# Re-dealt rows of the triangular inverses, rotation of two heads at once, split first loads and another stage order in a hybrid decoder block

## The chip, the cores and the metric

The kernel runs on one core of one Trainium2 chip. The metric is the device time of one execution in microseconds (us). TensorE (PE) does matrix products into PSUM; VectorE (DVE), ScalarE (ACT) and GpSimd (POOL) do everything else; transfers between HBM and on-chip memory (SBUF) are issued from the queues of SyncE (SP) and ScalarE.

## The reference

One decoder layer in float32, sequence 2048, model width 1024:

```
n    = rmsnorm(h);  proj = n @ w_in           # q,k,v,gate,a,b of 4 DeltaNet heads; q,k,v,gate of 4 retention heads
gdn:  silu(causal conv4(q,k,v)); l2norm(q), l2norm(k); chunks:
      T = (I + tril(beta k k^T * decay))^-1;  u = T v_beta - (T k_beta) S;  o = q S + (q k^T * decay) u;  S = d S + k^T u
ret:  q,k = rotary(q), rotary(k);  o = (q k^T * D) v + (q xi) R;  R = g R + (k zeta)^T v
mix  = [rms(o_gdn) * w * silu(gate), rms(o_ret) * silu(gate)]
h    = h + mix @ w_out
h    = h + (silu(g) * u) @ w_down,   g,u = causal conv3(rmsnorm(h) @ w_up)      # inner width 2816
out  = rmsnorm(h)
```

All heads are 128 wide. The rotary step multiplies a head's 128 columns by a cosine row and adds the columns with each two neighbours exchanged, times a sine row.

## The kernel before, in words

**Products.** Every float32 factor is split into a high and a low part, and a product runs as three passes: high·high, high·low, low·high (lines 116 to 118 in mm3; 399 to 401 in the token-major projections, tokmajor). The out projection (product, "wo") and the two MLP products are additionally done as seven half-size block products with sums instead of eight.

**Blocks and stages.** The sequence is cut in four blocks of 512 tokens, of four chunks of 128 each. Each block has some sixty mixer stages, named by a letter in ORDER (lines 41 to 51), which writes out their order by hand; a digit ahead is the block:

- pro: first norm. pro2 loads xT tiles (L382, on SP's queue) and scales each half into a high and a low part (L387 ScalarE, L388 VectorE); pro1 loads x and sums squares. load_chunk brings weights (L293 on SP), splits them (L295 ScalarE, L296 VectorE) and stores the split form in HBM for later blocks; `len(uses) > NLATE` leaves that out for the first NLATE chunks at their first use.
- k0, q0, kq, v0: the retention projections. rotate (L764 to L774) applies the rotary step per token tile and head pair: per head two VectorE products (L769, L771) out of PSUM and one POOL addition (L774).
- a, f: DeltaNet projections of a head; c: its k k^T and q k^T products (kk, L585) and the stores of the 32x32 diagonal blocks to HBM (z1, L621, on ScalarE's queue); e: v transposed; d, dec: decays.
- b0, b1: gdn_base, the inverses of the 32x32 diagonal blocks for a pair of heads. Nb is loaded from z1 (L628, SP), so that each of the 128 partitions holds one whole block. Each block is inverted by columns: POOL runs 31 times a product (L637) and an addition (L639). A block's 32 rows lie on four partitions, eight rows on each, and all eight are touched at every column. The result goes out to HBM as z2 in one 128 KB store (L641, SP), comes back in eight loads into a block-diagonal tile AT (L648, SP) and is transposed by VectorE into NT (L650).
- l0, l1: products that build the full 128x128 inverse from the 32x32 ones (yps, L665, is their first); r00 to r13: the recurrent steps of a pair of heads, chunk by chunk (gdn_rec: ks L714 → kv on VectorE L717 → wps L724 → u on VectorE L727 → sps L732 → state on VectorE L734).
- h, y: a retention head (rr L818, state steps L810, transposes L826, rkk L832; output ro L846, evacuated by ScalarE as o at L849, squares, power on POOL L857).
- p: gate projections (tokmajor again; ScalarE evacuates into mix, L412); g, G: o times norm and gate (VectorE, L435), transposed by TensorE (mxt, L437) and combined (co, L440 to L445).
- W1 to W7: the seven out-projection products (ScalarE and VectorE split the factor, L917 and L918; wo); N: second norm, transposed and stored to HBM (L952, L953).

The MLP follows: its input tiles xr are loaded from what N stored (SP, L985) and split by ScalarE (L973); the first tiles are prepared while block 3's mixers still run.

**What sets the order.** Each engine runs its instructions in one queue of its own, in program order. The program order comes from ORDER and, within and around it, from the framework's scheduler, which places instructions by their dependences. Tiles are drawn from pools; the numbers of buffers stand in BUFS and in NVR, NACC, NPB, NXR and others (lines 16 to 39). The pools' tiles share the bytes of SBUF as they come free, so a tile can wait for the last reader of another tile that lay there before it. The framework adds these waits.

**Constants.** cols (norm and conv weights), rows and masks (identity, triangle, and eye8, the start of the inverses) are loaded on ScalarE's queue (L95, L243, L248) at the start.

Of the kernel before, what the change touches and what calls it, by code (L numbers as in the profile page):

```python
# [10 lines left out]
AF = mybir.ActivationFunctionType  # L11
ALU = mybir.AluOpType
# [7 lines left out]
NVR = 4  # L20
# [4 lines left out]
NACC = 9  # L25
# [4 lines left out]
NPB = 11  # L30
# [3 lines left out]
NLATE = 3  # L34
NXR = 7
FD = 5
BUFS = {"n1": 8, "ykq": 5, "kv": 4, "NT": 6, "AT": 8, "o": 4, "n2s": 11, "xk": 2, "og": 1, "co": 7, "Cw": 7,
        "wx": 1, "wsq": 2, "wvr": 3, "wvt": 8, "ca": 8, "mix": 10, "D": 8, "rk": 6, "rq": 3, "rv": 8,
        "Ar": 1, "Nb": 7, "rot": 1, "rrow": 7}

ORDER = ("0pro 0k0 0v0 0dec 0d0 0a0 0c0 0f0 0e0 0q0 0d1 0a1 0c1 0f1 0a2 0e1 0d2 0c2 0f2 0h0 0y0 0b0 0h1 "
# [10 lines left out]
P = 128  # L52
S = 2048
D = 1024
KT = D // P
TB = 512
NB = S // TB
NT = TB // P
# [25 lines left out]
def hybrid_block(ctx, tc, x, xT, w_kq, w_v, w_g, w_rk, w_r0, w_r, w_o, w_u, w_d, cols, rows, fnr, masks, rot, out):  # L84
    nc = tc.nc
# [9 lines left out]
    nc.scalar.dma_start(colt, cols)  # L95
# [123 lines left out]
def mixers(ctx, tc, base, base_used, marks, drp, mm3, gamma, mhalf, n1w, n2w, gcw, gv127, epsr, gnw, n2d, hd,  # L219
# [28 lines left out]
    nc.scalar.dma_start(mk, masks)  # L248
# [6 lines left out]
    DVE.tensor_scalar(below, U, 1.0, 1e4, op0=ALU.subtract, op1=ALU.mult)  # L255
# [21 lines left out]

    def load_chunk(key, src):
        first = key not in uses
# [6 lines left out]
        for o in range(0, n, step):  # L286
# [3 lines left out]
            else:  # L290
                if o % (2 * step) == 0:
                    raw2 = unit(wp, "wraw", [P, 2, step], bufs=NRAW)
                    marks["w"] = nc.sync.dma_start(raw2.rearrange("p a n -> p (a n)"), src[:, o:o + 2 * step])  # L293
# [61 lines left out]
    def A_items(b, st):  # L355
# [22 lines left out]
        def pro2(_):  # L378
            st["n1"] = []
            for kk in range(4):  # L380
                xk = unit(ap_, "xk0", [P, 2, TB], bufs=4) if b == 0 else al("xk", [P, 2, TB])
                nc.sync.dma_start(xk.rearrange("p a t -> p (a t)"), xT[b, kk])  # L382
                for i in range(2):
# [3 lines left out]
                    ACT.activation(n1[:, 0], xk[:, i], AF.Copy, scale=n1w[:, k:k + 1])  # L387
# [237 lines left out]
        def gdn_base(p):  # L625
            def f(_):
# [8 lines left out]
                for j in range(31):  # L635
                    n = 31 - j
                    POOL.tensor_tensor(tm[:, :, :n], Nb[:, j:j + 1, j + 1:].to_broadcast([P, 8, n]),  # L637
                                      X[:, :, j:j + 1].to_broadcast([P, 8, n]), op=ALU.mult)
                    POOL.tensor_tensor(X[:, :, j + 1:], X[:, :, j + 1:], tm[:, :, :n], op=ALU.add)  # L639
                z2 = drp.tile([2, NT, 4, 32, 32], F32, tag="z2", name="z2")  # L640
                nc.sync.dma_start(z2.rearrange("h c k (g a) i -> (h c k g) (a i)", g=4), X.rearrange("p c i -> p (c i)"))  # L641
# [116 lines left out]
        def rot_dst(p, which):  # L758
            dst = [half(st, ("rt", p, which), "r" + which, i) for i in range(2)]
            for i in range(2):  # L760
                st["rh", 2 * p + i, which] = dst[i]
# [573 lines left out]
```

## Time and profile before

| | us |
|---|---|
| runs | 2462.69, 2459.72, 2457.21 |
| median | 2459.72 |
| span of the profiled execution | 2458.5 |
| TensorE busy | 2397.2 |
| VectorE busy | 1596.7 |
| ScalarE busy | 998.8 |
| POOL busy | 532.7 |

The profile is of one further execution; for it there is the span, from its first to its last instruction. Rows of instructions read: start in us, duration in us, engine, line, operation, output<-inputs, partitions x elements, count, and in brackets how long the engine was idle before and what released it. Rows of waits read: engine, tile and line that waited <- engine, tile and line that released it: us in all, times, longest. Rows of groups read: line, engine, operation, out<-in, shape, count | busy us, mean ns of one | idle us before them and what ended it. Rows of DMA kinds end with the size of one and the median us from issue to landing. The mixers of the four blocks end at about 1225 us; the rest is the MLP.

### The profile page before, as it was taken

To read this page: it belongs to the slowest core of one execution; us is meant where nothing else is said; L and a number is where in the kernel's file an instruction comes from. 1 tells how busy PE (TensorE), PEld (TensorE's weight loads), DVE (VectorE), ACT (ScalarE), POOL (GpSimd) and SP (SyncE) were. 2 spreads that over 40 slices of the span, in tenths; PEclk is the share of its full clock that TensorE was granted. 3 is DMA by queue.
4 is the path that set the end of the run, shared out by engine and by line. 5 is a ranking of instruction groups with operands and counts; after the bars stand their busy time and mean duration, and the time that the engine had idled before them with its cause. 6 is when DMAs were issued, how large, how long until landed. Compare 5 with 4: busy or idle time off the path is not lost.

```text
span 2458.5 us, 35801 instructions
## 1 busy us (share of the span) xinstructions
PE 2397.2 (98%) x12476; PEld 2016.0 (82%) x12476; DVE 1596.7 (65%) x3157; ACT 998.8 (41%) x2152; POOL 532.7 (22%) x877
## 2 busy tenths in 40 slices
PE   8998899999999999998999999999999999999998
PEld 7887788788888878887888888888888888888887
DVE  5855777444754563447888988896556577454674
ACT  6644535344442552336454344442122234332341
POOL 1354245621047105240000000000000002421030
PEclk9999999999999999999999999999999999999999
DMA  8856589674765656654998878877667778775773
GB/s 327 277 187 218 214 310 343 223 247 175 268 228 180 211 186 222 224 184 181 349 365 313 303 290 300 290 280 250 233 239 258 270 259 281 243 224 156 220 242 112
DMA packets 287477, 607.29 MB, mean 247 GB/s; under 512 B 41088, under 2 KB 121152, under 8 KB 287296
## 3 DMA queue, kind: packets, MB, share of 16 engines
q1 hardware_dynamic: 270720, 590.70, 68.7%
q10 hardware_dynamic: 16576, 14.30, 1.9%
q8 instruction: 98, 1.61, 0.3%
q14 instruction: 83, 0.68, 0.1%
HBM read 405.32 MB, written 199.59 MB: 246 GB/s over the span
## 4 chain that ended last, share of the span: by engine, by line
PE 84%; POOL 5%; DMA 4%; DVE 3%; issue 2%; ACT 2%; SPq 0%; ACTq 0%; POOLq 0%; DVEq 0%
PE p L116 11%; PE p L118 11%; PE p L117 11%; PE d L118 6%; PE d L116 6%; PE d L117 6%; PE tok L399 4%; PE tok L401 4%; PE tok L400 4%; PE chm L116 3%; PE chm L117 3%; PE chm L118 3%; POOL pers L639 2%; POOL pers L637 2%; PE wo L116 2%; PE wo L117 2%
## 5 line engine op out<-in xcount | busy, mean ns | idle before, releaser
L117 PE MATMUL p<-x,wu 128*128 128x512 f32 x1176 | 457.7, 389 | 0.0
L116 PE MATMUL p<-x,wu 128*128 128x512 f32 x1176 | 452.7, 389 | 0.0
L118 PE MATMUL p<-x,wu 128*128 128x512 f32 x1176 | 450.0, 389 | 0.0
L399 PE MATMUL tok<-wc,n 128*128 128x512 f32 (+2 forms) x768 | 276.5, 365 | 19.5 <-ACT n L387 9.6
L400 PE MATMUL tok<-wc,n 128*128 128x512 f32 (+2 forms) x768 | 276.6, 361 | 1.1 <-DVE wc L296 1.1
L401 PE MATMUL tok<-wc,n 128*128 128x512 f32 (+2 forms) x768 | 275.1, 361 | 0.0
L116 PEld LDWEIGHTS p<-x,wu 128*128 128x128 f32 x1176 | 220.8, 188 | 46.4 <-DVE uc L1053 0.4
L118 PEld LDWEIGHTS p<-x,wu 128*128 128x128 f32 x1176 | 220.8, 188 | 45.8
L117 PEld LDWEIGHTS p<-x,wu 128*128 128x128 f32 x1176 | 220.8, 188 | 45.8
L1095 DVE SCALAR_TENSOR_TENSOR acc<-uc,base,acc 128x1023 f32<-128x1023 f32 (+1 forms) x176 | 221.0, 1280 | 39.2 <-ACT acc L1092 38.9
L1053 DVE TENSOR_TENSOR uc<-p,uc 128x512 f32<-128x512 f32 x224 | 153.6, 689 | 134.8 <-PE p L118 131.6
L186 POOL TENSOR_TENSOR vt<-vr 128x512 f32<-128x512 f32 x44 | 66.0, 1504 | 633.0 <-DMA vr<-in_w_d 465.8
L399 PEld LDWEIGHTS tok<-wc,n 128*128 128x128 f32 x768 | 146.1, 191 | 41.0 <-ACT n L387 9.6
L117 PE MATMUL d<-v,uu 128*128 128x512 f32 x448 | 174.3, 389 | 0.0
L118 PE MATMUL d<-v,uu 128*128 128x512 f32 x448 | 174.3, 389 | 0.0
L116 PE MATMUL d<-v,uu 128*128 128x512 f32 x448 | 174.3, 389 | 0.0
L400 PEld LDWEIGHTS tok<-wc,n 128*128 128x128 f32 x768 | 146.5, 191 | 20.8 <-DVE wc L296 1.5
L401 PEld LDWEIGHTS tok<-wc,n 128*128 128x128 f32 x768 | 145.3, 191 | 19.8
L116 PE MATMUL chm<-n,wc 128*128 128x512 f32 x384 | 151.7, 395 | 0.0
L118 PE MATMUL chm<-n,wc 128*128 128x512 f32 x384 | 151.2, 394 | 0.0
L117 PE MATMUL chm<-n,wc 128*128 128x512 f32 x384 | 150.8, 393 | 0.0
L1092 ACT ACTIVATE acc<-uc,base 128x1024 f32<-128x1024 f32 x88 | 97.2, 1144 | 86.2 <-DVE uc L1053 45.1
(250 smaller groups left out, 4723.3 us busy)
## 6 DMA issues: line engine op xcount, KB each, us to landing
wu<-wu SPq DMA_DIRECT2D x308, 512.0 KB, 5.9
wc<-wd SPq DMA_DIRECT2D x168, 512.0 KB, 5.2
wv<-wo SPq DMA_DIRECT2D x84, 512.0 KB, 5.2
wd<-wc SPq DMA_DIRECT2D x60, 512.0 KB, 4.8
ur<-au SPq DMA_DIRECT2D x56, 512.0 KB, 5.5
wur<-in_w_u SPq DMA_DIRECT2D x44, 512.0 KB, 6.5
au<-st SPq DMA_DIRECT2D x88, 256.0 KB, 4.7
vr<-in_w_d SPq DMA_DIRECT2D x77, 256.0 KB, 5.0
```

The lines of the kernel that those rows point to most:

```text
L116: PE.matmul(ps, ah, bh, start=(first and i == 0), stop=False, skip_group_check=chk)
L117: PE.matmul(ps, ah, bl, start=False, stop=False, skip_group_check=chk)
L118: PE.matmul(ps, al, bh, start=False, stop=(i == n - 1), skip_group_check=chk)
L186: POOL.tensor_tensor(tt[:, j], a, b_, op=ALU.subtract)
L399: PE.matmul(ps, ah, wh, start=(k == 0), stop=False)
L400: PE.matmul(ps, ah, wl, start=False, stop=False)
L401: PE.matmul(ps, al_, wh, start=False, stop=(k == KT - 1))
L637: POOL.tensor_tensor(tm[:, :, :n], Nb[:, j:j + 1, j + 1:].to_broadcast([P, 8, n]), X[:, :, j:j + 1].to_broadcast([P, 8, n]), op=ALU.mult)
L639: POOL.tensor_tensor(X[:, :, j + 1:], X[:, :, j + 1:], tm[:, :, :n], op=ALU.add)
L1053: add = lambda o, ps, a: DVE.tensor_tensor(o, ps, a, op=ALU.add)
L1092: ACT.activation(acc, u, AF.Copy, scale=mcw[:, ci, 2:3])
L1095: DVE.scalar_tensor_tensor(acc[:, t:], u[:, :T2 - t], w, acc[:, t:], op0=ALU.mult, op1=ALU.add)
```

## The change

It has four parts.

1. **Inverse.** The 32 rows of a block are dealt to its four partitions in turn (row = 4a + g on partition g) instead of in runs of eight. At column j only the first j//4 + 1 of the eight places can hold anything but zero, and only these are multiplied and added. eye8 is dealt the same way. The z2 store becomes four, one for each g, of 32 KB in pieces of 32 numbers.
2. **Rotation.** Both heads of a pair at once: three VectorE instructions of 256 columns for each token tile and pair, the addition among them, in place of four of 128 on VectorE and two on POOL.
3. **First loads.** The first weight chunk and the first xT tile come in halves, interleaved on SP's queue; cols in a piece of 8 columns and the rest; the masks are issued behind the scale of the fourth half tile. NLATE goes from 3 to 4.
4. **Order.** A new ORDER string, and other buffer numbers. The MLP's code is the same, with NACC 9 to 8 and NXR 7 to 6.

```diff
--- before.py
+++ after.py
@@ -17,38 +17,38 @@
 LA = 1
 NHH = 5
 NUU = 14
-NVR = 4
+NVR = 5
 NVV = 23
 NWUR = 2
 NST = 4
 NUC = 6
-NACC = 9
+NACC = 8
 NWU = 9
 NWV = 5
 FX = (0, 2, 4, 1, 5)
 NU = 4
-NPB = 11
+NPB = 8
 NPM = 4
 NPR = 2
 NRAW = 3
-NLATE = 3
-NXR = 7
+NLATE = 4
+NXR = 6
 FD = 5
-BUFS = {"n1": 8, "ykq": 5, "kv": 4, "NT": 6, "AT": 8, "o": 4, "n2s": 11, "xk": 2, "og": 1, "co": 7, "Cw": 7,
-        "wx": 1, "wsq": 2, "wvr": 3, "wvt": 8, "ca": 8, "mix": 10, "D": 8, "rk": 6, "rq": 3, "rv": 8,
-        "Ar": 1, "Nb": 7, "rot": 1, "rrow": 7}
-
-ORDER = ("0pro 0k0 0v0 0dec 0d0 0a0 0c0 0f0 0e0 0q0 0d1 0a1 0c1 0f1 0a2 0e1 0d2 0c2 0f2 0h0 0y0 0b0 0h1 "
-         "0y1 0d3 0e2 0a3 0c3 0f3 0e3 0l0 0r00 0r01 0r02 0b1 0r03 0l1 0r10 0kq 0r11 0p1 0h2 0r12 0y2 "
-         "0r13 1pro 0p0 0g0 1k0 0h3 0G0 0y3 1dec 0g1 0G1 0W1 1d0 1a0 1c0 1f0 1e0 0W2 1a3 1q0 0W6 0W7 1d1 "
-         "1a1 1c1 1f1 1e1 1d3 1c3 0W5 1f3 1e3 1v0 0W3 1h1 1y1 1b0 1a2 0W4 1d2 1c2 1f2 1e2 1h0 1y0 1l0 0N "
-         "1kq 1r00 1r01 1r02 1b1 1h2 1y2 1r03 1p1 1p0 1l1 1r10 2pro 1h3 1y3 1r11 1g1 1r12 1r13 1g0 2k0 "
-         "1G1 2dec 1G0 2v0 1W1 1W2 2d0 2d2 2a0 2c0 2f0 2e0 1W6 1W7 2a2 1W5 1W3 2c2 2a1 2f2 2f1 2e2 1W4 "
-         "2d1 2c1 2e1 2b0 2q0 2h1 2y1 2d3 2a3 2c3 2f3 2b1 2e3 2h0 2y0 2l0 2r00 2r01 2p0 2r02 2r03 2l1 "
-         "2r10 2r11 2r12 2kq 2r13 2p1 1N 3pro 2g0 2h2 2y2 3k0 2h3 2y3 2G0 2g1 2G1 3dec 3d0 3a0 3c0 3f0 "
-         "3d1 3e0 2W1 2W2 2W6 3a2 3a1 3c1 3f1 3e1 2W7 3q0 3v0 3b0 3h0 3y0 2W5 3d2 3d3 3h1 3c2 3f2 3e2 "
-         "2W3 3a3 3c3 3kq 3y1 3f3 3e3 3p0 3l0 3r00 3r01 3r02 3r03 3h2 3y2 3b1 3l1 3r10 3r11 3r12 3r13 "
-         "3g0 2W4 3p1 3G0 2N 3h3 3y3 3g1 3G1 3W1 3W2 3W6 3W7 3W5 3W3 3W4 3N")
+BUFS = {"n1": 8, "ykq": 5, "kv": 5, "NT": 6, "AT": 9, "o": 7, "n2s": 16, "xk": 2, "og": 4, "co": 7, "Cw": 6,
+        "wx": 1, "wsq": 5, "wvr": 3, "wvt": 8, "ca": 7, "mix": 7, "D": 4, "rk": 8, "rq": 2, "rv": 9, "Ar": 1,
+        "Nb": 8, "rot": 1, "rrow": 8}
+
+ORDER = ("0pro 0k0 0v0 0dec 0d0 0a0 0c0 0f0 0e0 0d1 0a1 0c1 0f1 0a2 0e1 0q0 0d2 0f2 0h0 0c2 0y0 0b0 0h1 "
+         "0y1 0d3 0e2 0a3 0c3 0f3 0e3 0l0 0r00 0r01 0r02 0r03 0b1 0l1 0kq 0r10 0r11 0r12 0h2 0y2 0h3 0p1 "
+         "0r13 0p0 0g0 1pro 1k0 1dec 0y3 0g1 0G1 0W1 1a0 1f0 1d0 1c0 0W2 0G0 1a3 1e0 1d1 1q0 0W6 0W7 1a1 "
+         "1c1 1f1 1e1 0W5 1d3 1c3 1d2 1f3 1e3 1v0 0W3 1h1 1y1 1a2 0W4 1c2 1f2 1e2 1h0 1y0 1b0 1l0 0N 1r00 "
+         "1r01 1b1 1r02 1kq 1h2 1p1 1p0 1y2 1r03 1l1 1r10 1h3 1y3 2pro 1r11 1g1 1r12 1r13 1g0 2k0 2dec "
+         "2d0 1G0 2d2 2v0 1G1 1W1 2a0 2c0 1W2 2f0 1W6 1W7 2a2 1W5 2e0 1W3 2c2 2a1 2f2 1W4 2f1 2e2 2d1 2c1 "
+         "2b0 2e1 2q0 2h1 2y1 2d3 2a3 2c3 2f3 2b1 2e3 2h0 2y0 2l0 2r00 2r01 2p0 2p1 2r02 2r03 2l1 2r10 "
+         "2r11 2r12 2kq 2r13 1N 2h2 3pro 2g0 2y2 2h3 3k0 2y3 2G0 2g1 3dec 3a0 2G1 3d0 3c0 3f0 3v0 3e0 3a1 "
+         "2W1 3d1 2W2 2W6 3c1 3f1 2W7 3a2 3q0 3b0 3e1 2W5 3h0 3y0 3d2 3h1 3c2 3d3 3f2 2W3 3a3 3l0 3e2 3c3 "
+         "3y1 3f3 3e3 3b1 3r00 3kq 3p0 3r01 3r02 3h2 3y2 3l1 3r10 3g0 3r11 3r03 3G0 3r12 2W4 3r13 3p1 2N "
+         "3h3 3y3 3g1 3W1 3W2 3G1 3W6 3W7 3W5 3W3 3W4 3N")
 P = 128
 S = 2048
 D = 1024
@@ -92,7 +92,8 @@
     NCOL = cols.shape[1]
     base = cp.tile([P, U1], F32, name="base")
     colt = base[:, :NCOL]
-    nc.scalar.dma_start(colt, cols)
+    nc.scalar.dma_start(colt[:, :8], cols[:, :8])
+    nc.scalar.dma_start(colt[:, 8:], cols[:, 8:])
     n1w = colt[:, 0:8]
     n2w = colt[:, 8:16]
     gcw = colt[:, 16:64].rearrange("p (f t) -> p f t", t=4)
@@ -245,14 +246,17 @@
     dtb = rowt[:, 4:8]
 
     mk = pc(4, P)
-    nc.scalar.dma_start(mk, masks)
     ident = mk[:, 0, :]
     U = mk[:, 1, :]
     eye8 = mk[:, 2:].rearrange("p a b -> p (a b)").rearrange("p (c i) -> p c i", c=8)
 
 
     below = pc(P)
-    DVE.tensor_scalar(below, U, 1.0, 1e4, op0=ALU.subtract, op1=ALU.mult)
+
+    def constants(after):
+        with tc.issue_after(after.ins):
+            nc.scalar.dma_start(mk, masks)
+        DVE.tensor_scalar(below, U, 1.0, 1e4, op0=ALU.subtract, op1=ALU.mult)
     ones = pc(P)
     POOL.memset(ones, 1.0)
     phalf = pc(16)
@@ -275,8 +279,20 @@
     cache = {}
     uses = {}
 
+    x0 = {}
+
+    def first_x(kk, j=slice(0, 2)):
+        if kk not in x0:
+            x0[kk] = unit(ap_, "xk0", [P, 2, TB], bufs=4), []
+        xk, done = x0[kk]
+        if j not in done and slice(0, 2) not in done and len(done) < 2:
+            done.append(j)
+            sl = slice(j, j + 1) if isinstance(j, int) else j
+            nc.sync.dma_start(xk[:, sl].rearrange("p a t -> p (a t)"), xT[0, kk, :, sl.start * TB:sl.stop * TB])
+        return xk
+
     def load_chunk(key, src):
-        first = key not in uses
+        first, start = key not in uses, not uses
         uses[key] = uses.get(key, 0) + 1
 
         keep = not first or len(uses) > NLATE
@@ -290,7 +306,12 @@
             else:
                 if o % (2 * step) == 0:
                     raw2 = unit(wp, "wraw", [P, 2, step], bufs=NRAW)
-                    marks["w"] = nc.sync.dma_start(raw2.rearrange("p a n -> p (a n)"), src[:, o:o + 2 * step])
+                    for j in range(2) if start and o == 0 else (slice(0, 2),):
+                        a, n_ = (j, 1) if isinstance(j, int) else (0, 2)
+                        marks["w"] = nc.sync.dma_start(raw2[:, a:a + n_].rearrange("p a n -> p (a n)"),
+                                                       src[:, o + a * step:o + (a + n_) * step])
+                        if start:
+                            first_x(o // (2 * step), j)
                 raw = raw2[:, o // step % 2]
                 ACT.activation(wc[:, 0], raw, AF.Copy)
                 DVE.tensor_tensor(wc[:, 1], raw, wc[:, 0].bitcast(F32), op=ALU.subtract)
@@ -378,13 +399,16 @@
         def pro2(_):
             st["n1"] = []
             for kk in range(4):
-                xk = unit(ap_, "xk0", [P, 2, TB], bufs=4) if b == 0 else al("xk", [P, 2, TB])
-                nc.sync.dma_start(xk.rearrange("p a t -> p (a t)"), xT[b, kk])
+                xk = first_x(kk) if b == 0 else al("xk", [P, 2, TB])
+                if b:
+                    nc.sync.dma_start(xk.rearrange("p a t -> p (a t)"), xT[b, kk])
                 for i in range(2):
                     k = 2 * kk + i
                     n1 = al("n1", [P, 2, TB], F32R)
                     st["n1"].append(n1)
-                    ACT.activation(n1[:, 0], xk[:, i], AF.Copy, scale=n1w[:, k:k + 1])
+                    hi = ACT.activation(n1[:, 0], xk[:, i], AF.Copy, scale=n1w[:, k:k + 1])
+                    if b == 0 and k == 3:
+                        constants(hi)
                     DVE.scalar_tensor_tensor(n1[:, 1], xk[:, i], n1w[:, k:k + 1], n1[:, 0].bitcast(F32),
                                              op0=ALU.mult, op1=ALU.subtract)
 
@@ -633,12 +657,14 @@
                 tm = XX[:, 2 * P:4 * P].rearrange("p (c i) -> p c i", c=8)
                 POOL.tensor_copy(X, eye8)
                 for j in range(31):
-                    n = 31 - j
-                    POOL.tensor_tensor(tm[:, :, :n], Nb[:, j:j + 1, j + 1:].to_broadcast([P, 8, n]),
-                                      X[:, :, j:j + 1].to_broadcast([P, 8, n]), op=ALU.mult)
-                    POOL.tensor_tensor(X[:, :, j + 1:], X[:, :, j + 1:], tm[:, :, :n], op=ALU.add)
+                    n, m = 31 - j, j // 4 + 1
+                    POOL.tensor_tensor(tm[:, :m, :n], Nb[:, j:j + 1, j + 1:].to_broadcast([P, m, n]),
+                                      X[:, :m, j:j + 1].to_broadcast([P, m, n]), op=ALU.mult)
+                    POOL.tensor_tensor(X[:, :m, j + 1:], X[:, :m, j + 1:], tm[:, :m, :n], op=ALU.add)
                 z2 = drp.tile([2, NT, 4, 32, 32], F32, tag="z2", name="z2")
-                nc.sync.dma_start(z2.rearrange("h c k (g a) i -> (h c k g) (a i)", g=4), X.rearrange("p c i -> p (c i)"))
+                for g in range(4):
+                    nc.sync.dma_start(z2.rearrange("h c k (a g) i -> g (h c k) a i", g=4)[g],
+                                      X.rearrange("(b g) a i -> g b a i", g=4)[g])
                 for h in range(2):
                     hd_ = st["hd", 2 * p + h]
                     TT = hd_["TT"] = half(hd_, "at", "AT", 0)
@@ -756,22 +782,20 @@
             return f
 
         def rot_dst(p, which):
-            dst = [half(st, ("rt", p, which), "r" + which, i) for i in range(2)]
             for i in range(2):
-                st["rh", 2 * p + i, which] = dst[i]
-            return dst
+                st["rh", 2 * p + i, which] = half(st, ("rt", p, which), "r" + which, i)
+            return st["rt", p, which]
 
         def rotate(t, ps, dst):
             rt = st["rot"][:, t]
-            for i in range(2):
-                src = ps[:, i * P:(i + 1) * P]
-                tt = small("rt", P, 2)
-                DVE.tensor_tensor(tt, src, rt[:, 0, :], op=ALU.mult)
-                d = dst[i][:, t * P:(t + 1) * P]
-                DVE.tensor_tensor(d.rearrange("p (a s) -> p a s", s=2),
-                                  src.rearrange("p (a s) -> p a s", s=2)[:, :, ::-1],
-                                  rt[:, 1, :].rearrange("p (a s) -> p a s", s=2), op=ALU.mult)
-                POOL.tensor_tensor(d, d, tt, op=ALU.add)
+            pair = lambda v: v.rearrange("p (h s) -> p h s", s=P)
+            half2 = lambda v: v.rearrange("p h (a s) -> p h a s", s=2)
+            both = lambda k: rt[:, k, :].unsqueeze(1).to_broadcast([P, 2, P])
+            src, tt = pair(ps[:, :2 * P]), pair(small("rt", 2 * P, 2))
+            d = dst[:, :, t * P:(t + 1) * P]
+            DVE.tensor_tensor(tt, src, both(0), op=ALU.mult)
+            DVE.tensor_tensor(half2(d), half2(src)[:, :, :, ::-1], half2(both(1)), op=ALU.mult)
+            DVE.tensor_tensor(d, d, tt, op=ALU.add)
 
         def ret_k0(w):
             dst = rot_dst(0, "k")
@@ -798,7 +822,7 @@
             tokmajor(w, 512, evac)
 
         def ret_v(w):
-            dst = rot_dst(0, "v") + rot_dst(1, "v")
+            dst = [rot_dst(p, "v")[:, i] for p in range(2) for i in range(2)]
 
             def evac(t, ps):
                 for i in range(NH):
@@ -1259,7 +1283,7 @@
     m = np.zeros((P, 4, P), np.float32)
     m[:, 0] = np.eye(P)
     m[:, 1] = (i[:, None] <= i[None, :])
-    m[:, 2:] = np.eye(32, dtype=np.float32).reshape(4, 2, P)[i % 4]
+    m[:, 2:] = np.eye(32, dtype=np.float32).reshape(8, 4, 32).transpose(1, 0, 2).reshape(4, 2, P)[i % 4]
     lin = np.arange(64, dtype=np.float32) / np.float32(63)
     ang = np.repeat((np.float32(1.0) / np.power(np.float32(10000.0), lin)).astype(np.float32), 2)
     ph = np.arange(S, dtype=np.float32)[:, None] * ang[None, :]
```

Names in it: `unit` and `al` draw a tile from a pool, `half` draws one half of a tile shared by two users, `small` a small tile; `tc.issue_after` places an instruction behind another in its queue.

## The prediction

> **What bounds the kernel now.** I read the page's first part, then TensorE's waits (columns: total us, times, longest), then windows.
>
> ```profile
> span 2458.5 us, 35801 instructions
> PE 2397.2 (98%) x12476; PEld 2016.0 (82%) x12476; DVE 1596.7 (65%) x3157; ACT 998.8 (41%) x2152; POOL 532.7 (22%) x877
> PE tok L399 <- ACT n L387: 9.6, 1, 9.6
> PE sps L732 <- DVE pers L727: 6.4, 11, 0.9
> PE mxt L437 <- DVE mix L435: 5.8, 2, 5.0
> PE wps L724 <- DVE kv L717: 4.8, 8, 1.4
> 1225.00:2458.50 1233.50, 1226.53 (x5423) 1014.43 (x5421) 868.73 (x1202) 442.09 (x656) 125.27 (x116) 1.00 0.74 256
> ```
>
> TensorE is the bound: 2458.5 − 2397.2 = 61.3 us idle is all that a change of order or of another engine can give, beside stretches at half clock. The window from 1225 on (MLP; columns: length, then busy time of PE, PEld, DVE, ACT, POOL, then granted clock, DMA share, GB/s) leaves TensorE 1233.50 − 1226.53 = 7.0 us idle, nearly all at the end. So I look for idle time in the first half. The matrix products are the same number in both builds (11364), so the sum is made of gaps.
>
> **1. The start, −4.6 us.**
>
> ```profile
> 0.74 0.87 SPq L293 DMA_DIRECT2D wraw<-in_w_rk  x2
> 3.58 0.73 ACT L295 ACTIVATE wc<-wraw 128x264 fp32r<-128x264 f32 x2 [0.16 <-DMA wraw<-in_w_rk]
> 1.65 7.06 DMA xk<-in_xT
> 8.80 1.33 ACT L387 ACTIVATE n<-xk,base 128x512 fp32r<-128x512 f32 x2 [3.04 <-DMA xk<-in_xT]
> ```
>
> The first matmul waits for the first scaled xT tile (L387), whose transfer is the third on SP's queue, issued at 1.65 and 7.06 us on its way, with the constants and the masks beside it. After, its first half (256 KB) is issued ahead of or next to the first half chunk of weights at 0.74, the masks (256 KB) wait for the fourth scaled tile. The weights issued at 0.74 landed by 3.58, so the half tile lands near there (estimate 3.6 to 4.2); then one weight conversion (0.73 for two) and one scale (1.33 for two): first matmul at 5.0 instead of 9.57. Bounds: −2.5, if the split transfers share the engines so that all land late or the second tile is late next, to −5.5. Moving the masks costs nothing: their readers, the decay mask and the inverse's identity, belong to stages behind the first projections. Halving adds four small issues on SP and ACT at the start (0.4 us each by the row of two above), in the sum.
>
> **2. The inverse and the gates' wait in block 0, −7.7 us.**
>
> ```profile
> 155.27 1.02 PE L585 MATMUL kk<-ykq 128*128 128x256 f32 x4
> 177.09 0.62 POOL L637 TENSOR_TENSOR pers<-Nb,pers 128x248 f32<-128x248 f32 x1 [5.31 <-DMA Nb<-z]
> 217.47 0.22 POOL L639 TENSOR_TENSOR pers<-pers 128x8 f32<-128x8 f32 x1
>   ACT mix L412: 11.6, 1
> 212.88:218.31 5.43, 0.00 (x1) 0.00 (x0) 0.94 (x3) 0.89 (x3) 3.71 (x15) 0.79 0.00 0
> 218.31:222.90 4.59, 4.58 (x11) 3.62 (x12) 2.18 (x4) 3.58 (x9) 0.40 (x1) 0.50 0.21 49
> 156.30:212.88 56.58, 54.98 (x354) 44.67 (x353) 28.60 (x79) 17.15 (x51) 34.55 (x67) 1.00 0.69 245
> 143.16 0.34 POOL L639 TENSOR_TENSOR pers<-pers 128x80 f32<-128x80 f32 x1
> 143.58 0.32 POOL L637 TENSOR_TENSOR pers<-Nb,pers 128x72 f32<-128x72 f32 x1
> L637 POOL TENSOR_TENSOR pers<-Nb,pers 128x48 f32<-128x48 f32 x8 | 2.2, 278 | 0.6
> L637 POOL TENSOR_TENSOR pers<-Nb,pers 128x24 f32<-128x24 f32 x8 | 1.8, 226 | 0.6
> ```
>
> The order of events: the kk products end at 156.3; the inverse starts 20.8 us later (its input goes out to HBM and back as Nb) and runs to 217.7. ScalarE's gate evacuation (L412) waits 11.6 us for its last instruction, because the mix tile lies in Nb's bytes, and TensorE, which had 55.0 us of work in that stretch, then waits 5.43 us for the bank. Behind that gap 4.58 us of TensorE's work ran at a clock of 0.50, so another 2.3 us.
>
> The diff keeps 62 instructions per inverse but touches at column j only j//4+1 of 8 rows: 1560 elements per partition instead of 3968 over the 31 multiplies, on average 50, none over 80. At 278 ns (the 48-element form) and 0.08 between two (143.16 + 0.34 to 143.58): 62 × 0.36 = 22 us instead of 40.6. From above: before's forms would by the same line (226 ns at 24, 2 ns an element more) give 32 us, and 40.6 was measured, with other POOL work between; the same ratio makes 28. After, the built order has 175 wide matmuls and some 11 us of small ones between these events, 49 us of cover; 20.8 + 22 = 43 us, at worst 49. The wait goes: −5.43 − 2.3.
>
> [...]
>
> **3. The re-dealt store, in later waits.** One store of the inverse becomes four.
>
> ```profile
> z<-pers SPq DMA_DIRECT2D x8, 128.0 KB, 2.8
> z<-NT ACTq DMA_DIRECT2D x64, 16.0 KB, 4.1
> AT<-z SPq DMA_DIRECT2D x64, 16.0 KB, 1.9
> ```
>
> Before shows no store of this shape; its pieces are rows of 32 numbers (128 bytes), as in the second and third row. Bounds for the last of the four to land, with three issues of some 0.4 more on SP: 1.9 + 1.2 − 2.8 = +0.3 to 4.1 + 1.2 − 2.8 = +2.5; I take +1.7. Behind the first of them, SP's queue holds weight loads for the same time; DMA is no limit there (share 0.69).
>
> [...]
>
> **4. The second inverse of block 3, +2 us.** Here the new order works against it.
>
> ```profile
> 1022.53 1.02 PE L585 MATMUL kk<-ykq 128*128 128x256 f32 x4
> 1035.60 0.62 POOL L637 TENSOR_TENSOR pers<-Nb,pers 128x248 f32<-128x248 f32 x1 [11.73 <-DMA Nb<-z]
> 1075.62 0.22 POOL L639 TENSOR_TENSOR pers<-pers 128x8 f32<-128x8 f32 x1
> 1087.29 1.38 DVE L650 STREAM_TRANSPOSE NT<-AT 128x512 f32<-128x512 f32 x2 [3.74 <-DMA AT<-z]
> 1090.12 0.70 PE L665 MATMUL yps<-NT 128*32 128x32 f32 x32
> 1023.55:1090.12 66.57, 66.57 (x410) 54.83 (x408) 26.38 (x77) 17.03 (x40) 36.07 (x82) 1.00 0.67 221
> ```
>
> Before: 12 us to the inverse, 40.2 in it, 11.5 to the transposes, all under 66.6 us of products. After, the built order leaves 166 wide matmuls (0.217 us each, window below) and 5 us of small ones: 41 us. The chain becomes 12 + 22 + 5 to 14 (from below store and load of section 3, 2.8 + 1.9; from above this row's 11.5 and the 2.5 of section 3) = 39 to 50: a wait of 0 to 9. I take 2. The covers of the other pairs, counted the same way, are 58 and 57 (block 0), over 80 (block 1), 50 and 51 (block 2), 61 (block 3, first).
>
> **5. The end of block 3's mixers, −7.5 us.**
>
> ```profile
> 1150.19:1158.20 8.01, 6.92 (x21) 5.55 (x22) 8.01 (x19) 5.92 (x14) 0.00 (x0) 0.50 0.62 240
> 1145.52 0.63 ACT L973 ACTIVATE x<-xr 128x512 fp32r<-128x512 f32 x1 [1.16 <-DMA xr<-n2d]
> 1146.06 0.58 ACT L849 ACTIVATE o<-ro 128x512 f32<-128x512 f32 x1
> 350.00:360.00 10.00, 10.00 (x46) 8.29 (x45) 4.16 (x6) 1.27 (x2) 2.53 (x2) 1.00 0.89 266
> ```
>
> The last gate transpose (mxt) waits 5.0 us for o → mix (first fence); ScalarE's evacuation of o (L849) is queued behind an MLP tile's split (L973) that waits for a DMA. 6.92 us of work at 0.50 cost 3.46 more. In the built order 24 wo matmuls (24 × 10.00/46 = 5.2 us) stand between ro and this mxt, where none stood. −5.0 − 3.5 + 1 left = −7.5.
>
> **6. Recurrences and block tails, −6.5 us.**
>
> ```profile
> 247.00:290.00 43.00, 35.02 (x267) 31.62 (x266) 31.86 (x125) 27.25 (x76) 8.60 (x13) 1.00 0.51 192
> 865.00:890.00 25.00, 19.21 (x125) 16.34 (x125) 16.81 (x54) 14.09 (x46) 3.02 (x3) 1.00 0.45 154
> ```
>
> These stretches, the recurrent steps (L714 to L734) of block 0 and block 2's tail, leave TensorE 8.0 and 5.8 us idle. A step is a serial chain between TensorE and VectorE; it costs 0.4 to 0.9 us where no other product stands between its hops (first fence: 6.4 us over 11, 4.8 over 8). Counting in the built orders the hops with nothing between them: block 0's stretch loses 3 of 6 and part of its gate waits, −3; block 2's goes from 5 to 1, with projections ahead of the wo products, −4.5; block 3 has one or two more, +1. Range of the three: −10 to 0.
>
> **7. Rotation, 0.**
>
> ```profile
> L769 DVE TENSOR_TENSOR pers<-tok,rot 128x128 f32<-128x128 f32 x128 | 36.7, 287 | 51.2 <-PE tok L401 23.2 <-POOL rk L774 15.2 <-POOL rq L774 11.8
> L774 POOL TENSOR_TENSOR rq<-rq,pers 128x128 f32<-128x128 f32 x64 | 32.3, 519 | 16.2 <-DVE rq L771 9.2 <-PE tok L401 6.8 <-issue 0.2
> L443 DVE TENSOR_TENSOR co<-co 128x256 f32<-128x256 f32 x16 | 6.7, 421 | 0.2
> ```
>
> Per group 4 × 0.287 = 1.15 us on VectorE and 2 × 0.52 on POOL become 3 × 0.42 = 1.26 on VectorE: over 64 groups +7 on VectorE, −66 on POOL, and one hop between engines less. VectorE is busy 65% and the projections' products cover it; were the cover gone, at most 7. Lower bound: −2, where POOL's add stands ahead of an inverse.
>
> **8. What a new order costs that I cannot place, +4.** Of the 61.3 us idle, the named gaps (9.6, 5.4, 5.0, 8.0, 5.8) and the MLP's 7.0 leave some 20 us of small ones in the first half: weights, wu, first steps of a block. Every moved step takes its loads along on SP's queue, which issues 1457 DMAs instead of 1432 (24 of them section 3's), and tiles share other bytes with the new pool sizes. I count the same 20 us after and 4 more, from 0 to 10. The MLP does the same work with two buffers less and had no gaps: 0.
>
> **Sum.** −4.6 − 7.7 + 2 − 7.5 − 6.5 + 4 = −20.3 us: span 2438.2. The profiled execution's span lies 1.2 under the median of the runs (2459.72; 2457.21 to 2462.69), so 2439.4.
>
> **The rivals.**
> A. *Nothing new waits*: the +2, +1 and +4 fall away: 2432. For it: POOL loses 66 us of adds and 8 × 18 of inverse, and every chain in which it stands gets shorter. Against: most of those chains had cover.
> B. *The gap moves*: the transition's wait comes back behind another holder (+7.5) and block 3's chain takes its upper end (+7, and 2.3 of clock): −3.5, 2456, within 0.2% (4.9 us), which is about what a measurement of this kernel can tell from no change. For it: the transition is a chain of five engines' hops.
> C. *Slower: the inverse chains end after their shortened cover.* The place is the way behind the inverse (four stores, eight loads on SP's queue among weight loads). If kk to transposes lasts L, the waits are what L exceeds 41, 50, 51, 57, 58, 61. At L = 60: 19 + 10 + 9 + 3 + 2 = 43 and three half-clock stretches of 3 us, less the 2 counted: +50, 2489. It decides from about L = 54, where 13 + 4 + 3 and the clock (6) eat what was gained and 5 more. My L is 41 to 49; block 0's slow lead-in (20.8) with 28 and 5 gives 54 there, but against 57.
> D. *The inverse gains nothing*: small forms cost as much as large. Then L is 60 and the time that of C. Against: the row at 24 elements stands at 226 ns, the 248-element one at 620.
>
> **How the numbers follow.** Forecast 0.57, A 0.22, B 0.09, C 0.08, D 0.04. Faster by over 0.2% is forecast and A, 0.79; within, B, 0.09; slower, C and D, 0.12. The range 2426 to 2457 leaves out C, D, the upper half of B and a little of A.
>
> **What would show it.** First matmul near 5; an inverse of 22 to 28 us and no wait of tok on mix L412; the mxt wait near 1110 to 1150 under 2 us and no clock of 0.50 there; block 3's yps wait under 3; idle time of TensorE near 47 us instead of 61.3. A wait of yps or of ScalarE on POOL's inverse over 5 us, or a first matmul after 7, makes it wrong.

## The result and the profile after

| | median | runs | ratio to before, 95% interval |
|---|---|---|---|
| before | 2459.59 us | 2457.21 to 2462.69 | |
| changed | 2440.41 us | 2438.91 to 2442.43 | 0.9923 [0.9909, 0.9937] |

19.2 us faster (forecast 20.3). The profiled executions differ by 21.4 us, 2458.5 against 2437.1; all readings below are of profiles. The head of the changed kernel's page, and TensorE's waits (total us, times, longest):

```profile
span 2437.1 us, 35681 instructions
PE 2398.3 (98%) x12476; PEld 2018.5 (83%) x12476; DVE 1588.9 (65%) x3095; ACT 1000.5 (41%) x2152; POOL 401.3 (16%) x749
```

```profile
PE tok L423 <- ACT n L409: 5.3, 1, 5.3
PE sps L758 <- DVE pers L753: 4.4, 6, 1.7
PE rkk L856 <- ACT ykq L851: 4.1, 2, 3.4
PE p L117 <- ACT wu L997: 2.2, 1, 2.2
PE mxt L461 <- DVE mix L459: 1.4, 3, 1.1
PE tok L423 <- ACT mix L436: 1.2, 1, 1.2
```

TensorE's idle time falls from 61.3 to 2437.1 − 2398.3 = 38.8 us, and the busy time stays. The first wait is 5.3 instead of 9.6, the gates' (tok on mix) 1.2 instead of 5.4, mxt's 1.1 instead of 5.0. A wait of 3.4 (rkk) is new. The windows of the changed kernel at stretches like those of before (length, then busy time of PE, PEld, DVE, ACT, POOL, then clock, DMA share, GB/s):

```profile
136.00:240.00 104.00, 100.95 (x737) 85.58 (x736) 63.28 (x165) 54.13 (x150) 29.52 (x70) 1.00 0.69 242
240.00:276.00 36.00, 29.09 (x175) 26.23 (x174) 26.30 (x93) 19.02 (x52) 2.05 (x2) 0.76 0.50 185
276.00:860.00 584.00, 578.32 (x3507) 496.78 (x3506) 329.53 (x891) 249.46 (x691) 151.77 (x321) 1.00 0.70 243
860.00:885.00 25.00, 25.00 (x138) 21.67 (x137) 5.14 (x17) 7.89 (x31) 1.76 (x2) 1.00 0.47 153
1085.00:1205.00 120.00, 109.58 (x560) 90.40 (x559) 91.10 (x185) 63.14 (x144) 6.94 (x9) 0.99 0.70 260
```

and of the kernel before, where not shown yet:

```profile
140.00:247.00 107.00, 97.62 (x684) 82.13 (x683) 59.32 (x151) 46.94 (x136) 50.74 (x110) 0.97 0.65 227
290.00:865.00 575.00, 564.88 (x3436) 484.01 (x3434) 326.53 (x902) 249.50 (x679) 220.51 (x384) 1.00 0.70 242
1100.00:1225.00 125.00, 113.50 (x625) 96.45 (x624) 98.19 (x208) 66.14 (x160) 7.38 (x9) 0.96 0.68 257
```

Idle time by stretch, before → after: start 9.6 → 5.3; the middle of block 0 9.4 → 3.1; its end 8.0 → 6.9; blocks 1 and 2 10.1 → 5.7; block 2's tail 5.8 → 0; block 3's end 11.5 → 10.4; the MLP 7.0 both. But the end of block 0 now has a mean granted clock of 0.76, where it was 1.00.

### The profile page after: what moved, and what is told of

Same layout as the page of the kernel before. It is cut to its first block, busy times and chain, and to the rows that moved or that the text cites. A ratio compares the mean times of both kernels' runs of the same rounds, so it can differ in the third digit from the quotient of the medians.

```text
span 2437.1 us, 35681 instructions
## 1 busy us (share of the span) xinstructions
PE 2398.3 (98%) x12476; PEld 2018.5 (83%) x12476; DVE 1588.9 (65%) x3095; ACT 1000.5 (41%) x2152; POOL 401.3 (16%) x749
## 4 chain that ended last, share of the span: by engine, by line
PE 82%; POOL 7%; DMA 4%; issue 2%; DVE 2%; SPq 1%; ACT 1%; ACTq 0%; POOLq 0%; DVEq 0%
PE p L117 11%; PE p L119 11%; PE p L118 11%; PE d L119 6%; PE d L117 6%; PE d L118 6%; PE tok L423 4%; PE tok L424 4%; PE tok L425 4%; POOL pers L663 3%; POOL pers L661 3%; PE chm L119 3%; PE chm L117 3%; PE chm L118 3%; PE wo L117 2%
## 5 line engine op out<-in xcount | busy, mean ns | idle before, releaser
L1119 DVE SCALAR_TENSOR_TENSOR acc<-uc,base,acc 128x1022 f32<-128x1022 f32 (+1 forms) x176 | 221.1, 1279 | 39.8 <-ACT acc L1116 39.7
```

The source lines that it names most:

```text
L1119: DVE.scalar_tensor_tensor(acc[:, t:], u[:, :T2 - t], w, acc[:, t:], op0=ALU.mult, op1=ALU.add)
```

## The experiments

First, one part at a time is undone in the changed kernel: the inverse (e1), the rotation (e2), the first loads (e3), the order with the buffer numbers (e4). Ratios are to the kernel before, with 95% intervals. Of the code, only the lines that matter are shown.

**e1**, the old inverse:

```diff
-n, m = 31 - j, j // 4 + 1            # and its four stores, eye8
+n = 31 - j                           # all eight rows, one store
```

> The changed kernel with the inverse as it was before (all eight rows at each column, one store), everything else as changed. Theory: the new order leans on the short inverse. The inverse grows from 23-29 us to 35-40, its end-to-use chain by some 12, and the covers that the new order leaves (some 50 us of TensorE work in block 0 and block 2, 41 in block 3's second pair) are passed in four to six places by 5 to 14 us, some of it at half clock: 2470 to 2495 us, slower than the kernel before (2459.6). Rival: the covers are longer than counted and only block 0's wait of the gates comes back (5 us and 2.3 of clock): 2447 to 2450.

2472.26 us, 1.0051 [1.0036, 1.0066]. The size is the theory's, the places are not: the gates' wait is 4.0, and the one yps wait, which should have been among the largest, is 0.7 us; the others are mostly waits of recurrent steps in block 0 and one of 6.4 in the MLP, at 1256.

**e2**, the old rotation (four on VectorE, two additions on POOL):

```diff
-DVE.tensor_tensor(d, d, tt, op=ALU.add)            # both heads, 256 columns
+POOL.tensor_tensor(d, d, tt, op=ALU.add)           # for each head, 128 columns
```

> The changed kernel with the rotation as it was before (four instructions on VectorE and two additions on POOL for a token tile and pair). Theory (the prediction's): rotation is worth nothing, 2438 to 2443; POOL gets some 60 us more work, the inverses a few us longer where the additions fall between their columns. Rival, seen in the trace of the changed kernel at 247 to 253 us: the rotation's additions stand on VectorE ahead of the recurrent step's u and state, TensorE waits 1.7 and 1.3 us and runs at half clock for some 10 us behind it; with the additions on POOL that stretch keeps its clock: 2432 to 2437.

2463.29 us (ten runs, 2457.6 to 2467.9), 1.0014 [1.0005, 1.0024]: 23 us slower than the changed kernel, against both.

**e3**, the old first loads:

```diff
-first_x(o // (2 * step), j)                        # halves, xT's first; masks behind k == 3
+nc.sync.dma_start(xk.rearrange("p a t -> p (a t)"), xT[b, kk])    # whole, behind the weights; masks first
```

> The changed kernel with the first loads as before (no halves, masks and cols first). Theory: the start is serial, the whole 4.3 us comes back: first matmul near 9.6, 2444 to 2446. Rival: the first projections are fed by the DMA engines anyway, so a late start is caught up within the first stage by fewer waits: 2440 to 2442.

2478.3 us, 1.0076 [1.0061, 1.0091]: 38 us for a start that comes 3.9 later. TensorE's waits in e3, line numbers some 24 lower than in the changed kernel:

```profile
PE tok L399 <- ACT n L387: 9.2, 1, 9.2
PE p L116 <- ACT wu L973: 9.0, 2, 6.4
PE sps L734 <- DVE pers L729: 8.3, 8, 3.1
PE wps L726 <- DVE kv L719: 7.7, 7, 3.4
```

The first row is the part's own price. The others lie from 144 us on, and no first load ends them.

**e4**, order and buffer numbers as before, the three other parts new:

```diff
-ORDER = ("0pro 0k0 0v0 0dec 0d0 0a0 0c0 0f0 0e0 0d1 ...     # and NVR, NACC, NPB, NLATE, NXR, BUFS
+ORDER = ("0pro 0k0 0v0 0dec 0d0 0a0 0c0 0f0 0e0 0q0 ...
```

> The kernel before, its order and buffer numbers kept, with the three other parts (inverse, rotation, first loads). Theory: start -4.3 and block 0's gate wait -7.7 come without the new order, the wait at the end of block 3's mixers (5 us and 3.5 of clock) and block 2's tail stay: 2446 to 2449. Rival: the inverse's end is not what holds the gates in the old order once POOL is free (another tile's last reader takes its place), so only the start is gained: 2454 to 2456.

2469.59 us, 1.0044 [1.0029, 1.0059], *slower* than before. The start is gained (first matmul at 5.4) and the gates' wait shrinks to 1.7, but the old order meets a dozen other waits of 1 to 3 us, and the one ahead of mxt is 6.5.

So each part undone costs 23 to 38 us, far more than its terms in the prediction. What these runs have in common is the plan, the order that the scheduler gives all instructions: it is rebuilt from the edit on. In the traces, the first instruction that differs from the changed kernel's stands at 103 us in e1 (the first inverse) and at 31 in e2 (the first rotation). The longest run of VectorE's instructions in common order, gaps allowed, is 89% of the changed kernel's in e1, 85% in e2 and 91% in e3. The next runs keep the plan nearly as it is: in e5 nothing differs ahead of 1028 us, and 3057 of VectorE's 3095 instructions are of the same kind as the one at that place in the changed kernel.

**e5**, one long inverse, in block 3's second pair:

```diff
-n, m = 31 - j, j // 4 + 1
+n, m = 31 - j, 8 if (b, p) == (3, 1) else j // 4 + 1
```

> The changed kernel with one of the eight inverses long: block 3's second pair works on all eight rows at each column (zeros included; the layout and the four stores stay). The instruction order of all engines up to there is the same as in the changed kernel, and nearly the same behind it. Theory (the prediction's price of a late chain): the inverse takes 23 us now and some 35 then; its chain from the last kk to yps, 42.6 us without a wait, becomes 55 and passes the cover of some 41 to 45 by 10 to 13, with 3 us of half clock: 2453 to 2457 (2440.4 now). Rival: the scheduler puts block 3's gate products ahead of the late yps, and only hops that these covered come bare: 2441 to 2445.

2442.58 us, 0.9927 [0.9911, 0.9942]: the rival, and by these intervals no different from the changed kernel. The timelines of e5, the last kk, the inverse's first and last instruction and the first yps, and a window over them:

```profile
1019.53 1.03 PE L609 MATMUL kk<-ykq 128*128 128x256 f32 x4
...
1075.38 0.70 PE L691 MATMUL yps<-NT 128*32 128x32 f32 x32
```

```profile
1028.86 0.62 POOL L661 TENSOR_TENSOR pers<-Nb,pers 128x248 f32<-128x248 f32 x1 [6.57 <-DMA Nb<-z]
...
1060.76 0.22 POOL L663 TENSOR_TENSOR pers<-pers 128x8 f32<-128x8 f32 x1
```

```profile
1020.00:1095.00 75.00, 75.00 (x465) 63.18 (x463) 33.01 (x89) 22.42 (x65) 31.98 (x68) 1.00 0.53 180
```

The chain is 54.8 us instead of 42.6, and TensorE is busy in all of the 75 us: the scheduler put 187 gate products (tok) ahead of yps where there were 144, and more recurrent steps. A cover counted in one plan is no limit in the next.

**e6**, the old rotation in block 3 alone:

```diff
+if b == 3:
+    for i in range(2):                      # the four VectorE products of before
+        ...
+        POOL.tensor_tensor(d[:, i], d[:, i], tt[:, i], op=ALU.add)
+    return
```

> The changed kernel with the rotation as before (additions on POOL) in block 3 alone; the order of TensorE is the same up to block 3. Theory: rotation by itself is worth nothing in either direction, 2438 to 2443, and the 23 us of the run with the old rotation everywhere came from the re-planned order, not from rotation. Rival: additions on POOL cost time wherever they stand ahead of an inverse or a state step, a quarter of those 23 us: 2445 to 2448.

2448.47 us, 0.9951 [0.9934, 0.9968], 8 us slower: the rival's time. From block 3's first norm product to the first MLP product the profile has 321.2 us instead of 316.0. The two inverses of block 3 take 28.8 and 28.3 us instead of 26.6 and 22.9, with 3.7 and 7.6 us of additions (L801) between their columns; yet yps waits for neither. The time goes at another place, in VectorE's and SP's timelines of e6:

```profile
980.18 0.69 DVE L921 TENSOR_TENSOR Cw<-Cw,wx 128x512 f32<-128x512 f32 x1 [1.93 <-DMA wx<-in_x]
980.79 0.70 DVE L676 STREAM_TRANSPOSE NT<-AT 128x512 f32<-128x512 f32 x1
981.42 0.25 DVE L841 SCALAR_TENSOR_TENSOR pers<-pers,rr 128x128 f32<-128x128 f32 x1
```

```profile
971.35 0.52 SPq L666 DMA_DIRECT2D z<-pers  x1
...
976.71 0.44 SPq L926 DMA_DIRECT2D wx<-in_x  x1
```

The addition that waits for the load wx (L921) now stands ahead of a retention state step (L841); in the changed kernel it stands behind it. The load itself is issued behind the inverse's stores, the first of which leaves SP's queue at 971.35 instead of 964.00. TensorE's rr waits 2.6 us for this, with 3.4 us at half clock behind it: 4.3 of block 3's 5.2 us. Whether the late inverse or the new order weighs more here isn't separated. Where block 3 starts, e6's profile is already 2.6 us behind the changed kernel's and e5's 4.9, with the same order of instructions up to there; that much is no effect of the edit.

**e7 and e8** go at the end of block 0, where the changed kernel's two timelines read (VectorE, then TensorE):

```profile
248.29 0.68 DVE L317 TENSOR_TENSOR wc<-wraw,wc 128x512 fp32r<-128x512 f32 x1
248.88 0.42 DVE L796 TENSOR_TENSOR pers<-tok,rot 128x256 f32<-128x256 f32 x1
...
249.68 0.41 DVE L798 TENSOR_TENSOR rk<-rk,pers 128x256 f32<-128x256 f32 x1
250.01 0.42 DVE L753 TENSOR_TENSOR pers<-wps,pers 128x256 f32<-128x256 f32 x1
```

```profile
250.49 0.71 PE L758 MATMUL sps<-pers,kv 128*128 128x128 f32 x4 [1.72 <-DVE pers L753]
...
252.89 2.08 PE L740 MATMUL ks<-pers,ykq 128*128 128x128 f32 x8 [1.25 <-DVE pers L760]
```

The recurrent step's u (L753) stands behind a weight split and block 1's rotation, the addition (L798) among it.

```diff
-1pro 1k0 1dec 0y3 0g1 0G1 0W1 1a0 1f0
+1pro 1k0 1a0 1dec 0y3 0g1 0G1 0W1 1f0      # e7
+1pro 1a0 0y3 0g1 0G1 1k0 1dec 0W1 1f0      # e8
```

> The changed kernel with one stage moved in the order: block 1's first DeltaNet projection (1a0, 48 wide products) directly behind 1k0, ahead of 0y3, 0g1 and 0G1, so that its products fall between the last recurrent hops of block 0, where TensorE was busy 40% of the time at 248 to 253 us and then ran at half clock to 262 and again at 269 to 275. Theory: the clock falls where the busy share of some 4 us is low; filling two hops removes 3 us idle and 4 us of half clock at least: 2430 to 2435. Rival: the same hops come bare a little later, and the waits of the wo products move with them: 2438 to 2443.

2443.52 us, 0.9927 [0.9909, 0.9946]: just above the rival's range. The half clock at 252 to 262 is gone, but one wait of 5.5 us (wps on ScalarE's evacuation of o) comes at 271.

> The changed kernel with block 1's 1k0 and 1dec behind 0G1 and 1a0 ahead of 0y3. Beside e7's products, the rotation and the weight splits of 1k0 leave VectorE's queue where it holds the recurrent step's u and state. Theory: idle at block 0's end falls from 6.9 to 3 us and the first half-clock stretch (4 us lost) goes: 2430 to 2434. Rival: the stages of block 1 behind it lose the products taken away and stall there: 2439 to 2446.

2438.5 us, 0.9911 [0.9895, 0.9927]: between the two ranges; faster than before, and not to be told from the changed kernel by these intervals. Windows of e8:

```profile
240.00:276.00 36.00, 30.69 (x243) 29.03 (x242) 28.50 (x98) 20.70 (x58) 3.20 (x4) 1.00 0.54 182
```

The clock there is 1.00 instead of 0.76, as the theory had it; the idle time (5.3 us, 6.9 in the changed kernel) hardly falls, and later places give back some of it.

**e9**, an edit without a price of its own:

```diff
-if b == 0 and k == 3:
+if b == 0 and k == 4:
     constants(hi)
```

> The changed kernel with the masks issued behind the fifth scaled half tile instead of the fourth. Nobody needs them within tens of us, so the edit has no price of its own; it moves the scheduler's plan a little (the instruction in TensorE's queue is the same kind at 10844 of 11366 places, VectorE's at 2731 of 3097). Theory: the 13 to 38 us that undoing any one part cost come from the re-planned order, which the order string and the buffer numbers no longer fit; then this edit costs several us too: 2445 to 2475. Rival: they come from the parts themselves, and an edit without a price leaves 2438 to 2443.

2462.35 us (ten runs, 2455.9 to 2465.6), 1.0008 [0.9998, 1.0018]: the theory. All of the gain is gone, with 96% of VectorE's instructions in common order. The masks land at 19.2 us instead of 15.8; TensorE first reads them at 37, and up to 145 us its products run within 1 us (median) of the changed kernel's. By 450 they are 13 us late, by 500 15, at the end 18.4. So the edit has no price where it stands. Waits of e9:

```profile
PE wps L750 <- DVE kv L743: 7.0, 7, 3.5
PE sps L758 <- DVE pers L753: 6.7, 7, 2.8
PE yps L691 <- DVE NT L676: 4.0, 3, 2.1
PE kqtr L579 <- DVE Cw L914: 2.5, 1, 2.5
```

The waits of the recurrent steps (wps, sps) are longer than in the changed kernel, those of yps and kqtr are new, and the start is as it was (first matmul at 5.35).

**e10**, whole first loads, the rest of part 3 kept:

```diff
-for j in range(2) if start and o == 0 else (slice(0, 2),):
+for j in (slice(0, 2),):
```

> The changed kernel with the first weight chunk and the first xT tile whole again, all else of the first loads as changed. By the start alone the first matmul comes 1 to 2.5 us later: 2441.5 to 2443 (theory: a part's own price shows where the plan stays near). Rival: the re-planned order (2618 of 3097 places the same on VectorE) costs more than the start: 2448 to 2478, as in the run with all old first loads.

2472.19 us, 1.005 [1.0035, 1.0065]: the rival; the first matmul comes only 0.4 us later (5.74), so halving the tiles is the smallest part of what the start gained.

**e11 and e12**, on the kernel before: the inverse alone (the reverse of e1's edit), and the order and buffer numbers alone (the reverse of e4's):

> The kernel before with the new inverse alone. Theory (the prediction's second term): block 0's gates stop waiting for it, 5.4 us and 2.3 of half clock go: 2451 to 2453 (2459.7 now). Rival: the scheduler re-plans with the shorter inverse and the old order does not fit that plan: 2458 to 2475, with the gates' gap gone and others in its place.

2468.1 us, 1.0038 [1.0025, 1.0052]: the rival; the gates still wait 3.6 us.

> The kernel before with the new order and buffer numbers alone. Theory: the order brings block 2's tail and the end of block 3's mixers (some 9 us by the two traces) but its shorter covers meet the old inverse's 35 to 40 us, as in the run with the old inverse: 2462 to 2485. Rival: the order pays by itself, 2445 to 2452.

2461.86 us, 1.0004 [0.9994, 1.0014]: near the theory's lower end; no difference from before.

One sum holds them together. Idle time is the span less TensorE's busy time; beside it stands the length of the stretches with a granted clock of 0.50 (but for the last, idle one). About half of that is lost where TensorE is busy: in the changed kernel eight products of ks take 2.08 us at a clock of 0.50 (from 252.89) and 1.06 at 1.00 (from 264.92).

| kernel | span | idle | at half clock | span − idle − half of that |
|---|---|---|---|---|
| before | 2458.5 | 61.3 | 17.0 | 2388.7 |
| changed | 2437.1 | 38.8 | 23.8 | 2386.4 |
| e3 | 2478.6 | 69.3 | 47.7 | 2385.5 |
| e8 | 2435.0 | 42.6 | 6.8 | 2389.0 |
| e9 | 2455.5 | 52.3 | 30.6 | 2387.9 |
| e11 | 2465.5 | 65.6 | 17.0 | 2391.4 |

In all 14 kernels the last column is 2384 to 2392. So the differences here are TensorE's idle time and half clock, to within that spread of 7 us. Most lie before the MLP; but e1, e3 and e10 have a wait of 6.4 us early in it, with 6.8 to 10.2 us at half clock from there.

## Why the prediction was right, point by point

The time came out within 1 us (2440.4 against 2439.4). That closeness is luck: the terms were off by up to 9 us each and cancelled. The direction and the size rest on terms 1, 2 and the tail of block 2, which came nearly as counted.

1. *Start, −4.6*: −4.25 (first matmul at 5.32). Right. By e10, 0.4 of it is the halving; the rest comes with xT's earlier issue, the split cols and the later masks, which no run separates.
2. *Gates, −7.7*: −4.2 and the clock's 2.3. The wait shrank to 1.2 instead of going. The inverse takes 27 us, near the upper bound, not 22, and it starts 22.6 us behind the last kk instead of 20.8: 49.7 us against a cover counted as 49. The timeline of POOL in the changed kernel, and what ScalarE's gate evacuation waits for:

```profile
171.28 0.24 POOL L661 TENSOR_TENSOR pers<-Nb,pers 128x31 f32<-128x31 f32 x1 [17.24 <-DMA Nb<-z]
...
185.09 0.81 POOL L661 TENSOR_TENSOR pers<-Nb,pers 128x68 f32<-128x68 f32 x1
...
198.20 0.22 POOL L663 TENSOR_TENSOR pers<-pers 128x8 f32<-128x8 f32 x1
```

```profile
198.15 1.57 ACT L436 ACTIVATE mix<-tok,pers 128x256 f32<-128x256 f32 x4 [4.96 <-POOL pers L661]
```

   The 128x68 multiplication takes 0.81 here and 0.31 in six of the other seven inverses; the mean of a form hides this. The eight inverses take 22.9 to 29.4 us. ScalarE's 4.96 us stand at the very edge of the 5 that the prediction named as a sign of being wrong.
3. *Stores, +1.7*: from the inverse's end to the first transpose 7.0 to 9.5 us, median 7.8, against 5.0 to 12.8, median 6.5, before: +1.3. Each store lands in 2.0 us (median), the lower end of the two bounds; the issues cost more than I put, 0.6 each instead of 0.4.
4. *Block 3's second inverse, +2*: 0. Its lead-in was 8.5 us, not 12, the chain 42.6, with no wait. The prediction's sum is off here: 12 + 22 + 14 make 48, not 50, and with its own upper bound of 28 for the inverse 54, a wait of up to 13. (Rival C's turning point leaves out the 2 us already counted: 26 − 2 is 3.7 more than the gain, not 5.)
5. *The end of block 3's mixers, −7.5*: about −2.9 (idle 11.5 → 10.4; half clock 10.2 → 3.4 us, some 3.5 → 1.7 lost). mxt's wait went as forecast, but the first MLP product waits 2.2 us there, and seven recurrent hops of 0.4 to 0.8 us at 1095 to 1107 stand bare. The "1 left" and the +1 for block 3's recurrences were too small.
6. *Tails, −6.5*: block 2's −5.8 (forecast −4.5); block 0's −1.1 idle but 17 us at half clock where there were none: +7 on the other side. The step failed in one assumption of mine, which terms 4 and 8 share and no run shows: that a wait under 3 us costs only itself. The largest gap there is 1.72 us, and 10.24 us at a clock of 0.50 stand behind it.
7. *Rotation, 0*: not settled. In e6 block 3 takes 5.2 us more, outside the −2 that I gave as the lower end, but 4.3 of them come at a place where VectorE's order had changed too. On the other side the addition moved to VectorE stands ahead of u at 250. e2 cannot price it, as its plan differs.
8. *New stalls, +4*: blocks 1 and 2 lost 4.4 us of idle time and gained 1.7 of clock loss, so about −3; the middle of block 0 lost 2 more beside the gates' wait; the MLP 0, as forecast. So −5 stands against +4: these 9 us paid for terms 5 and 6.

The measured terms add up to −18.6 of the 21.4 us between the two profiles; the table's last column has 2.3 more.

In all idle time fell by 22.5 us (my terms: 14.5) and half clock rose by 6.8 us, which costs 3 to 4 (my terms: 5.8 gained). Rival C did not come: in the changed kernel no yps waits more than 0.4 us, and e5 shows that its fixed cover was the wrong picture.

The experiments refute most clearly that the gain is a sum over the four parts: e4, e11 and e12 give none of it, and e9 loses it by an edit worth nothing. Single waits do follow their part. The first matmul comes at 5.3 to 6.0 in every kernel with the new first loads, e10 included, and at 9.2 to 9.9 in every other. The total does not follow. The prediction counted on the built order of this very kernel, where covers and hops can be read; e4 and e11 were expected from the parts, with the same terms, and came out wrong. That this way of counting made the difference is argued, not shown: e7 and e8, whose gains were counted in the changed kernel's timeline, came out 8.5 and 4.5 us above their theories. e9 is a single control. Why this order suits this one plan so much better than its neighbours isn't settled by these runs.

## What to carry to other kernels

Where a scheduler places the instructions, undoing a part prices the new plan with it: first put in an edit that costs nothing and see how far the time moves (here 22 us). Count on the built order of the kernel that will run, engine by engine, and vary one local place late in the program, so that the plan ahead of it stays. Look at TensorE's busy share over a few us and not only at its longest gap: here a share of 0.40 over 3.41 us, with no gap over 1.72, stood ahead of 10.24 us at half clock.

## What the hardware showed that I had not expected

Half clock also came where TensorE had no long gap but was little busy. But for the idle one at the end, the stretches at 0.50 last 10.24, 6.83, 3.41 and 3.41 us in the changed kernel, 6.83 and 10.24 in the one before, that is one to three times 3.41 us. In each of the two profiles their starts lie whole multiples of 3.41 us apart (251.96, 269.03, 494.31 and 1139.42; 216.06 and 1147.90). Windows cut in these steps, of the changed kernel and of the one before:

```profile
248.55:251.96 3.41, 1.37 (x10) 0.97 (x9) 3.41 (x11) 0.85 (x2) 0.00 (x0) 1.00 1.02 411
251.96:262.20 10.24, 8.26 (x35) 7.70 (x36) 7.78 (x35) 6.29 (x16) 1.05 (x1) 0.50 0.27 104
265.60:269.01 3.41, 1.78 (x12) 1.16 (x10) 2.20 (x9) 1.64 (x7) 1.01 (x1) 1.00 0.39 119
269.01:275.85 6.84, 5.58 (x16) 4.37 (x17) 6.32 (x22) 4.00 (x8) 0.00 (x0) 0.50 0.29 98
1095.10:1098.51 3.41, 1.94 (x13) 1.52 (x12) 2.11 (x7) 1.43 (x6) 0.00 (x0) 1.00 0.00 0
1098.51:1101.92 3.41, 2.75 (x20) 2.42 (x20) 1.74 (x7) 1.02 (x6) 0.00 (x0) 1.00 0.00 0
```

```profile
267.30:270.71 3.41, 1.72 (x15) 1.52 (x15) 2.84 (x16) 3.38 (x6) 1.80 (x4) 1.00 0.00 0
270.71:274.12 3.41, 3.41 (x33) 3.41 (x32) 2.02 (x10) 2.24 (x10) 0.00 (x0) 1.00 0.01 2
```

A share of 1.37/3.41 = 0.40 is followed by half clock, and so is one of 0.52; 0.57 and 0.50 are not. e9 has 0.40 once more (1.35 of the 3.41 us from 250.54), with 10.24 us at 0.50 behind it. With both profiles cut into such steps, without start and tail, a step at full clock had half clock behind it in 5 of 5 cases with a share up to 0.40 (0.08, 0.36 and 0.40 in the changed kernel, 0.07 and 0.19 in the one before), in 1 of 7 between 0.50 and 0.58, and in none above. What decided between those 7 stays open. Behind a step at half clock, the next was at half again in the 6 cases with a share of 0.33 to 0.81, and at full clock in the 6 with 0.92 to 1.00. So one thin step can cost several: the three from 251.96 have shares of 0.61, 0.81 and 1.00, and no gap ahead of them was over 1.72 us.

The start is slow as well, though no record of the clock says so: there is none before 9.61 us in the changed kernel. Its matmuls of 264 columns start 0.22 us apart up to there and 0.12 behind it. From the first matmul this lasts 4.3 us in the changed kernel (from 5.32) and 5.1 in the one before (from 9.57).
